# A two-layer transformer forward pass on one core: blocks of the attention's output projection put between the last head's stages, the gating layer's mixing and transposes cut into steps, and its gate vector's products spread over 44 work units instead of 62

## The chip, the core and the metric

The kernel runs on 1 core of one Trainium2 chip. The metric is the device time of one execution in microseconds (us), taken as the median of several runs. The core's engines work at the same time and wait for each other through semaphores: TensorE (PE in the profile, its weight loads PEld) multiplies matrices, VectorE (DVE) and ScalarE (ACT) work element by element, GpSimd (POOL) does a few cross-partition operations, SyncE (SP) issues most DMAs. Matmuls write PSUM; everything else lies in SBUF.

## The reference

256 latent tokens of width 2048 pass two layers. Each layer has a mixer and a feed-forward part; each of the four sub-layers is modulated by six vectors worked out from a condition (`ada_params`) and ends in a gated residual and a layer norm. Layer 0 mixes by neighbourhood attention with 16 heads, layer 1 by the gated MLP below.

```python
def spatial_gating_mlp(a, w_in, ln_g, ln_b, w_s, b_s, w_out):
    u, v = jnp.split(jax.nn.gelu(a @ w_in, approximate=False), 2, axis=-1)
    v = layer_norm(v, ln_g, ln_b).reshape(bsz, n // CHUNK, CHUNK, N_GROUPS, GROUP_DIM)
    v = jnp.einsum("gpq,bkqgc->bkpgc", w_s, v) + jnp.transpose(b_s)[:, :, None]
    return (u * v.reshape(bsz, n, D_MODEL)) @ w_out
...
    sh1, sc1, g1, sh2, sc2, g2 = ada_params(c[:, None, :], ada_w[i], ada_b[i])
    a = modulate(h, sh1, sc1)
...
    h = layer_norm(ALPHA * h + g1 * y, ln_g[i, 0], ln_b[i, 0])
    h = layer_norm(ALPHA * h + g2 * swiglu(modulate(h, sh2, sc2), ffn_w_in[i], ffn_w_out[i]),
                   ln_g[i, 1], ln_b[i, 1])
```

## The kernel before, in words

**Matmuls.** Every large product of 32-bit numbers is made of three matmuls in a rounded 32-bit format (`mm3`, L85 to L88): high part by high part, high by low, low by high. Operands are split into the two parts by an ACT copy (L91) and a DVE subtraction (L92).

**Pieces.** Weights come in pieces of 128x1024 numbers (512 KB). SP issues their DMAs into 4 raw buffers, `prefetch` (L104) splits them (tiles `hw…` and `lw…`) into a ring of 5 buffers from the feed-forward part on, and so the split of a piece stands up to four pieces ahead of its matmuls. One piece feeds 12 matmuls of 128x512. In the gating layer the pieces are named `wg` (two input halves) and `wgo` (output projection), in the feed-forward part `wf` and `wd`, in the attention's output projection `wo`.

**Conditioning tasks.** The vectors from `ada_params` are made in small DVE steps beside the matmuls. A gate vector such as (1, G1), the one that scales the gating layer's output, takes 32 products of 128x1024 on DVE (`gate_task`, L174), each with a 512 KB DMA issued from ACT's queue, and then one `partition_all_reduce` on POOL (`sum_task`, L189) that adds over the 128 partitions. `pace(n)` (L230) spreads the tasks that are queued over n ticks; `block_T` and the output projections call `tick` (L214) once for each piece. A tick with an entry in the list `side` runs that entry and counts 0.3. What is left when the vector is wanted is done at once (`need`, L226).

**Attention (L595 to L604).** After each head's projections its stages (scores, an empty one, transposes, values) wait in the list `pend`; after the last head they are emptied in a row (L603). Then `project_out` (L718) runs the output projection in two halves `nh`; in the first, each piece gives 12 matmuls and a tick.

**Gating layer (L873 to L929).** Four chunks of 8 pieces make v (tiles `gv`), four chunks of 8 pieces make u (tiles `gu`), each chunk through `block_T` (L784) and a Gelu on ACT. Behind chunk nb of u, `spatial` (L896) runs twice for chunk nb-1: four mixing matmuls (L904, tile `sp`), a DVE step on each that adds a bias and multiplies into u (L905), transposes on PE (L909, tile `uvt`) and an ACT copy. The last chunk's two calls are side entries of the output projection `go`. `block_T` takes a list `turn` of extra steps; from its third piece on it runs one behind each piece. The feed-forward part uses that for its own transposes (L819).

A scheduler of the framework reorders independent instructions across and within the engines by its own priorities; the order of the text is where it starts. `keep_in_program_order` fixes the DMAs and the conditioning products.

Of the kernel before, what the change touches and what calls it, by code (L numbers as in the profile page):

```python
# [15 lines left out]
ALU = mybir.AluOpType  # L16
# [3 lines left out]
P = 128  # L20
# [26 lines left out]
W0 = HK0 * P + 512  # L47
EARLY = tuple((3 + 4 * g + h, h, 4 * g) for g in range(3) for h in range(4))
EN = 4
EARLY_END = {HK0 + h: 12 for h in range(4)}  # L50


@with_exitstack
def hybrid_kernel(ctx: ExitStack, tc: tile.TileContext, i, out):
# [175 lines left out]
    def pace(units):  # L230
        state["rate"] = sum(t[1] for t in tasks) / units
# [43 lines left out]
    with tc.tile_pool(name="attnX", bufs=1) as px, ExitStack() as late:  # L275
# [202 lines left out]
        def acc_tile(name):  # L478
            return mp.tile([P, 512], F32, tag="acc", name=name, bufs=4)

        def s_tile(name):
            return mp.tile([P, 512], F32, tag="s", name=name, bufs=2)

        def t_tile(name):
            return mp.tile([P, 512], F32, tag="t", name=name, bufs=2)

        add_tasks(0, SH2, SC2, G1)
        pace(126)
        pend = []
        with tc.tile_pool(name="attnB", bufs=1) as pb:  # L490
            qh, ql = {}, {}

            def advance():
                stage = pend.pop(0)
                if stage:
                    stage()
# [36 lines left out]
            def proj_v(g):  # L533
                ps = [acc_tile(f"vps{g}{b}") for b in range(4)]
                for k2 in range(8):
                    hi, lo = piece()
                    for kk in range(2):
                        kt = k2 * 2 + kk
                        c = slice(kk * 512, (kk + 1) * 512)
                        for b in range(4):  # L540
                            tb = slice(b * P, (b + 1) * P)
                            mm3(ps[b], ah[:, kt, tb], al[:, kt, tb], hi[:, c], lo[:, c], kt == 0, kt == KT - 1)
                    unit(2.0)
                for b in range(4):
                    put_v(g, b, ps[b])
# [49 lines left out]
            for h in range(NH):  # L595
                if h >= HK0:
                    proj_k(h)
                proj_q(h)
                if h in V_AT_Q:
                    while len(pend) > 8:  # L600
                        advance()
                    proj_v(V_AT_Q[h])
            while pend:  # L603
                advance()  # L604

    need((0, SH2), (0, SC2))
    main = ctx.enter_context(tc.tile_pool(name="main", bufs=1))
# [107 lines left out]
    QUIET = 2  # L715
    AHEAD = 400

    def project_out(kts, src, key, name, finish, extra, last=False):  # L718
        st = stats_tile(name)
        hold = LAST if last else HOLD  # L720
        for nh in range(2):
            if nh == 0:
                ps = [[acc_tile(f"po{name}{nh}{n}{b}") for b in range(2)] for n in range(2)]
            else:
                ps = [[s_tile(f"po{name}{nh}0{b}") for b in range(2)]]
                ps.append([acc_tile(f"po{name}{nh}1{b}") for b in range(2)])

            def products(kt, x, w, n, b):
                c, tb = slice(n * 512, (n + 1) * 512), slice(b * P, (b + 1) * P)
                mm3(ps[n][b], x[0][:, tb], x[1][:, tb], w[0][:, c], w[1][:, c], kt == 0, kt == kts - 1)  # L730

            def fetch(kt, n):
                xs = []
                for k in range(n):
                    at = None
                    if k >= START:
                        if k % 2 == 0:
                            e = outer.tile([P, 4, NT], F32R, tag="ada", name=f"e{name}{k}", bufs=ADA)
                        at = e[:, 2 * (k % 2), :], e[:, 2 * (k % 2) + 1, :]
                    xs.append(act_split(src(kt + k), f"{name}{nh}_{kt + k}", at))  # L740
                return xs, take(n)

            k0 = 0
            if nh == 1:
                xs, ws = fetch(0, START)
                for n in range(2):
                    for j in range(START):
                        for b in range(2):
                            products(j, xs[j], ws[j], n, b)
                preload_sqrt(st)  # L750
                k0 = START
            k1 = kts - hold if nh == 1 else kts
            for kt in range(k0, k1):
                if nh == 1 and kt == max(k1 - 9, k0):
                    pos["extra"] = extra()
                w = piece() if nh == 0 or kt < k1 - START else take(1)[0]
                x = act_split(src(kt), f"{name}{nh}_{kt}")
                for n in range(2):
                    for b in range(2):
                        products(kt, x, w, n, b)  # L760
                if nh == 0 or kt < k1 - QUIET:
                    tick()
            if nh == 0:
                need(key)
                g = gate[key]
                for n in range(2):
                    for b in range(2):
                        residual(ps[n][b], b, n, g, st, name)
            else:
                xs, ws = fetch(k1, hold)  # L770
                for b in range(2):
                    for n in range(2):
                        for j in range(hold):
# [34 lines left out]
    def ffn(layer, m, key, name, finish, free, last=False):  # L808
# [45 lines left out]
    project_out(  # L854
        KT, lambda k: oT[:, k, :], (0, G1), "wo", m.first,
        lambda: pw.tile([P, 4, 1024], F32R, tag="w", name="extra_o"),
    )
    affine_tasks(h_t, i["ln_row"][0], "a0")
    add_tasks(0, G2)
# [13 lines left out]
    m = m2[0]  # L873
    affine_tasks(h_t, i["ln_row"][1], "a1")
    add_tasks(1, G1)
    pace(62)
    free = ExitStack()
    pg = free.enter_context(tc.tile_pool(name="gm", bufs=1))
    ws = pg.tile([P, NH, P], F32, tag="ws", name="ws")
# [13 lines left out]
    uT = outer.tile([P, KT, NT], F32, tag="xT", name="uT")  # L893
    us = {}

    def spatial(nb, g2):  # L896
        u = us[nb]
        tp = t_tile(f"uvt{nb}{g2}")
        sp = s_tile(f"sp{nb}{g2}")
        for j in range(2):  # L900
            g = nb * 4 + g2 * 2 + j
            c = slice((g2 * 2 + j) * P, (g2 * 2 + j + 1) * P)
            o = sp[:, j * NT : (j + 1) * NT].rearrange("p (b c) -> p b c", b=2)
            T.matmul(o, ws[:, g, :], vv[:, :, g * P : (g + 1) * P], start=True, stop=True)  # L904
            V.scalar_tensor_tensor(u[:, :, c], o, bs[:, g : g + 1], u[:, :, c], ALU.add, ALU.mult)  # L905
        for j in range(2):
            c = slice((g2 * 2 + j) * P, (g2 * 2 + j + 1) * P)
            for b in range(2):
                T.transpose(tp[:, j * NT + b * P : j * NT + (b + 1) * P], u[:, b, c], ident)  # L909
        S.copy(uT[:, nb * 4 + g2 * 2 : nb * 4 + g2 * 2 + 2, :], tp)  # L910

    for nb in range(NB):
        ps = [acc_tile(f"gu{nb}{b}") for b in range(2)]
        if nb == 0:
            rs = [moments(b, st, "v")[1] for b in range(2)]
            affine_tasks(vv, i["gm_row"], "av", rs)
        block_T(m, ps, False)
        us[nb] = pg.tile([P, 2, 512], F32, tag="u", name=f"u{nb}", bufs=2)
        for b in range(2):
            S.activation(us[nb][:, b, :], ps[b], AF.Gelu)  # L920
        if nb:
            for g2 in range(2):
                spatial(nb - 1, g2)
    side.extend((lambda: spatial(NB - 1, 0), lambda: spatial(NB - 1, 1)))
    m = Modulated(2, 1, SH2, SC2, "f1")
    project_out(
        KT, lambda k: uT[:, k, :], (1, G1), "go", m.first,
# [135 lines left out]
```

## Time and profile before

| | |
|---|---|
| Median of 3 runs | 2418.88 us (2416.48 to 2419.06) |
| The profiled execution's own time | 2419.84 us |
| Its span in the profile | 2418.1 us |
| PE busy | 2381.7 us, 98% |
| DVE busy | 1755.7 us, 73% |
| ACT busy | 1122.7 us, 46% |
| POOL busy | 109.8 us, 5% |

All times are microseconds from the start of the profiled span. In a row of the timeline the first number is the start, the second the duration (for a group the stretch or the sum), then engine, line, operation, output and inputs; behind `x` the number of instructions, and in brackets the idle time of the engine ahead of it and what ended it. Matmuls are pipelined, so the distance between two starts is what one costs. Stages of the gating layer: v from about 1400, its chunks ending at 1411, 1432, 1454 and 1476; u's chunks ending at 1498, 1519, 1548 and 1573; the output projection behind that.

### The profile page before, as it was taken

The numbers are of one execution on the slowest core, as the hardware profiler recorded it, in microseconds if no ns is written. First come the engines' busy times: TensorE is split into PE (matmuls) and PEld (weight loads), VectorE is DVE, ScalarE is ACT, GpSimd is POOL, SyncE is SP. The second block draws the span as 40 slices with busy tenths as digits, with TensorE's granted clock in tenths as the row PEclk, the third lists the DMA queues.
The fourth block names the chain that finished last, engine by engine and source line by source line (L and its number), as shares of the span: only waits on it lengthen the run. The fifth ranks groups of instructions, "written<-read, shape, count | busy, mean of one in ns | idle before, by whom it ended". The sixth has DMA issues, their size and how long they took to land. (4 is left out here: it accounts for less than half of the span.)

```text
span 2418.1 us, 31362 instructions
## 1 busy us (share of the span) xinstructions
PE 2381.7 (98%) x11624; PEld 1977.0 (82%) x11624; DVE 1755.7 (73%) x2155; ACT 1122.7 (46%) x1536; POOL 109.8 (5%) x55
## 2 busy tenths in 40 slices
PE   9999999999999999999999999999999999999998
PEld 6788988888788888888888788777888888888886
DVE  4877867677788877777889788787755555576666
ACT  4344534345644444444445554446544444445553
POOL 0000000020010200000000011020100000020000
PEclk9999999999999999999999999999999999999999
DMA  9977877756679899999989677756766677656563
GB/s 382 346 265 239 272 240 238 244 164 209 197 267 338 302 334 318 320 319 320 329 287 321 202 247 270 271 177 200 235 228 228 226 233 225 207 186 195 176 212 132
DMA packets 167827, 610.64 MB, mean 253 GB/s; under 512 B 19349, under 2 KB 21717, under 8 KB 163317
## 3 DMA queue, kind: packets, MB, share of 16 engines
q1 hardware_dynamic: 121172, 440.74, 54.3%
q10 hardware_dynamic: 46372, 167.86, 20.1%
q8 instruction: 91, 1.49, 0.3%
q14 instruction: 64, 0.52, 0.1%
q0 software_dynamic: 128, 0.03, 0.0%
HBM read 606.46 MB, written 2.10 MB: 252 GB/s over the span
## 5 line engine op out<-in xcount | busy, mean ns | idle before, releaser
L92 DVE TENSOR_TENSOR lwf<-rwf,hwf 128x1024 fp32r<-128x1024 f32 x320 | 407.2, 1275 | 278.9 <-ACT hwf L91 278.6
L91 ACT CAST hwf<-rwf 128x1024 fp32r<-128x1024 f32 x320 | 337.1, 1054 | 490.5 <-PE pu L88 221.6
L86 PE MATMUL pod<-hwd,ghd 128*128 128x512 f32 x684 | 266.4, 390 | 0.0
L87 PE MATMUL pod<-lwd,ghd 128*128 128x512 f32 x684 | 266.2, 389 | 0.0
L88 PE MATMUL pod<-hwd,gld 128*128 128x512 f32 x684 | 265.8, 389 | 0.0
L92 DVE TENSOR_TENSOR lwd<-rwd,hwd 128x1024 fp32r<-128x1024 f32 x172 | 212.2, 1235 | 64.0 <-ACT hwd L91 63.8
L150 DVE SCALAR_TENSOR_TENSOR ad<-ad,c_bc 128x1024 f32<-128x1024 f32 x192 | 232.6, 1219 | 0.6 <-DMA ad<-in_ada_t 0.6
L91 ACT CAST hwd<-rwd 128x1024 fp32r<-128x1024 f32 x172 | 180.6, 1050 | 54.8 <-PE pod L88 28.8
L174 DVE SCALAR_TENSOR_TENSOR gate<-ag,c_col,gate 128x1024 f32<-128x1024 f32 x128 | 163.2, 1282 | 0.0
L88 PEld LDWEIGHTS pod<-hwd,gld 128*128 128x128 f32 x684 | 128.3, 188 | 26.8
L86 PEld LDWEIGHTS pod<-hwd,ghd 128*128 128x128 f32 x684 | 128.4, 188 | 26.7 <-DVE sg L838 0.3
L87 PEld LDWEIGHTS pod<-lwd,ghd 128*128 128x128 f32 x684 | 128.4, 188 | 26.6
L86 PE MATMUL pg<-hwf,f1h 128*128 128x512 f32 x320 | 126.4, 395 | 0.0
L86 PE MATMUL pg<-hwf,f0h 128*128 128x512 f32 x320 | 126.4, 395 | 0.0
L87 PE MATMUL pg<-lwf,f0h 128*128 128x512 f32 x320 | 124.6, 389 | 0.4 <-DVE lwf L92 0.4
L88 PE MATMUL pg<-hwf,f1l 128*128 128x512 f32 x320 | 124.7, 390 | 0.0
L88 PE MATMUL pg<-hwf,f0l 128*128 128x512 f32 x320 | 124.7, 390 | 0.0
L86 PE MATMUL pu<-hwf,f0h 128*128 128x512 f32 x320 | 124.5, 389 | 0.0
L87 PE MATMUL pu<-lwf,f0h 128*128 128x512 f32 x320 | 124.5, 389 | 0.0
L88 PE MATMUL pu<-hwf,f0l 128*128 128x512 f32 x320 | 124.5, 389 | 0.0
L86 PE MATMUL pu<-hwf,f1h 128*128 128x512 f32 x320 | 124.5, 389 | 0.0
L87 PE MATMUL pu<-lwf,f1h 128*128 128x512 f32 x320 | 124.5, 389 | 0.0
(343 smaller groups left out, 5338.5 us busy)
## 6 DMA issues: line engine op xcount, KB each, us to landing
rwf<-in_w_in_t SPq DMA_DIRECT2D x320, 512.0 KB
ad<-in_ada_t ACTq DMA_DIRECT2D x192, 512.0 KB
rwd<-in_w_out SPq DMA_DIRECT2D x176, 512.0 KB
ag<-in_ada_g ACTq DMA_DIRECT2D x128, 512.0 KB
rwg<-in_w_gin SPq DMA_DIRECT2D x64, 512.0 KB
ap<-in_ada_p SPq DMA_DIRECT2D x20, 1024.0 KB
rwq<-in_w_q SPq DMA_DIRECT2D x32, 512.0 KB
rwo<-in_w_o SPq DMA_DIRECT2D x32, 512.0 KB
```

The costliest lines, as they stand in the source:

```text
L86: keep(T.matmul(ps, sh, mh, start=first, stop=False))
L87: keep(T.matmul(ps, sh, ml, start=False, stop=False))
L88: keep(T.matmul(ps, sl, mh, start=False, stop=last))
L91: S.copy(hi, src)
L92: V.tensor_tensor(lo, src, hi.bitcast(F32), ALU.subtract)
L150: pin(V.scalar_tensor_tensor(r, r, 1.0, c_bc[:, half * 1024 : (half + 1) * 1024], ALU.mult, ALU.mult, accum_out=o[:, nt : nt + 1],))
L174: pin(V.scalar_tensor_tensor(g, loaded.pop(key), c_col[:, kt, 0:1], g, ALU.mult, ALU.add))
```

## The change

Three edits. First, the first half of an output projection becomes a pair made by `out_begin` (accumulators, and a step that does one piece), which `project_out` uses for all its callers. For the attention it is made ahead of the place where the last head's stages are emptied: two blocks run when three stages are left and one when one is left (`WHILE`). Second, `spatial` returns four steps, two that mix and two that transpose; they are handed to the `block_T` of the next chunk, so that mixing of chunk nb-1 runs behind pieces 2 and 3 (counted from 0) of chunk nb and the transposes behind pieces 4 and 5, where before both ran behind piece 7. The last chunk's four steps are side entries. Third, the 32 products of gate (1, G1) are paced over 44 units, not 62.

```diff
+WHILE = {3: 2, 1: 1}
...
+        def out_begin(kts, src, name):
+            ps = [[acc_tile(f"po{name}0{n}{b}") for b in range(2)] for n in range(2)]
+
+            def step(kt):
+                w = piece()
+                x = act_split(src(kt), f"{name}0_{kt}")
+                for n in range(2):
+                    c = slice(n * 512, (n + 1) * 512)
+                    for b in range(2):
+                        tb = slice(b * P, (b + 1) * P)
+                        mm3(ps[n][b], x[0][:, tb], x[1][:, tb], w[0][:, c], w[1][:, c], kt == 0, kt == kts - 1)
+                tick()
+
+            return ps, step
...
+            wo_ps, wo_step = out_begin(KT, lambda k: oT[:, k, :], "wo")
+            wo_k = 0
             while pend:
                 advance()
+                for _ in range(WHILE.get(len(pend), 0)):
+                    wo_step(wo_k)
+                    wo_k += 1
...
-                ps = [[acc_tile(f"po{name}{nh}{n}{b}") for b in range(2)] for n in range(2)]
+                ps, step, k0 = begun or (*out_begin(kts, src, name), 0)
+                for kt in range(k0, kts):
+                    step(kt)
...
-    pace(62)
+    pace(44)
...
-    def spatial(nb, g2):
+    def spatial(nb):
         u = us[nb]
...
+        def mix(g2):
+            sp = s_tile(f"sp{nb}{g2}")
...
+                T.matmul(o, ws[:, g, :], vv[:, :, g * P : (g + 1) * P], start=True, stop=True)
+                V.scalar_tensor_tensor(u[:, :, c], o, bs[:, g : g + 1], u[:, :, c], ALU.add, ALU.mult)
+
+        def turn(g2):
+            tp = t_tile(f"uvt{nb}{g2}")
...
+        return [partial(f, g2) for f in (mix, turn) for g2 in range(2)]
...
-        block_T(m, ps, False)
+        block_T(m, ps, False, spatial(nb - 1) if nb else ())
...
-        if nb:
-            for g2 in range(2):
-                spatial(nb - 1, g2)
-    side.extend((lambda: spatial(NB - 1, 0), lambda: spatial(NB - 1, 1)))
+    side.extend(spatial(NB - 1))
```

**First place: DVE in the last chunk of u, with the last products of the gate.** `gate<-ag` is one of the 32 products, `lwg` and `lwgo` are the low parts of pieces, `u<-sp` is the bias and product on a mixed block. Before, DVE's rows from the last piece of that chunk on:

```order
L92 TENSOR_TENSOR lwg_1024_13494<-rwg_1024_13491,hwg_1024_13493 128x1024
L92 TENSOR_TENSOR lwgo_0_0_13512<-rwgo_0_0_13509,hwgo_0_0_13511 128x1024
L174 SCALAR_TENSOR_TENSOR gate_12253<-ag_13306,c_col,gate_12253 128x1024
L92 TENSOR_TENSOR lwgo_0_1024_13533<-rwgo_0_1024_13530,hwgo_0_1024_13532 128x1024
L92 TENSOR_TENSOR lwgo_1_0_13551<-rwgo_1_0_13548,hwgo_1_0_13550 128x1024
L174 SCALAR_TENSOR_TENSOR gate_12253<-ag_13345,c_col,gate_12253 128x1024
L174 SCALAR_TENSOR_TENSOR gate_12253<-ag_13450,c_col,gate_12253 128x1024
L92 TENSOR_TENSOR lwgo_1_1024_13572<-rwgo_1_1024_13569,hwgo_1_1024_13571 128x1024
L905 SCALAR_TENSOR_TENSOR u_13404<-sp_13591,bs,u_13404 128x2x128
L905 SCALAR_TENSOR_TENSOR u_13404<-sp_13602,bs,u_13404 128x2x128
```

Now, the rows from piece 5 of the same chunk on; the gate row among them is the last of the 32:

```order
L93 TENSOR_TENSOR lwg_1024_13474<-rwg_1024_13471,hwg_1024_13473 128x1024
L175 SCALAR_TENSOR_TENSOR gate_12253<-ag_13353,c_col,gate_12253 128x1024
L93 TENSOR_TENSOR lwg_0_13493<-rwg_0_13490,hwg_0_13492 128x1024
L929 SCALAR_TENSOR_TENSOR u_13447<-sp_13508,bs,u_13447 128x2x128
L93 TENSOR_TENSOR lwg_1024_13516<-rwg_1024_13513,hwg_1024_13515 128x1024
L929 SCALAR_TENSOR_TENSOR u_13447<-sp_13508,bs,u_13447 128x2x128
L929 SCALAR_TENSOR_TENSOR u_13447<-sp_13532,bs,u_13447 128x2x128
L93 TENSOR_TENSOR lwgo_0_0_13540<-rwgo_0_0_13537,hwgo_0_0_13539 128x1024
L929 SCALAR_TENSOR_TENSOR u_13447<-sp_13532,bs,u_13447 128x2x128
```

The products of the gate end inside chunk 3 of u now, where before eight more followed in the output projection behind the rows shown; POOL's reduction becomes free to start behind the last one, one low part ahead of the first mixed block's step.

**Second place: PE in the same chunk.** `gu` are the chunk's accumulators, `sp` the mixing matmuls. Now, from the end of piece 2 on:

```order
L89 MATMUL gu_13451<-hwg_0_13412,m1l 128x512
L928 MATMUL sp_13508<-vv,ws 128x256
L87 MATMUL gu_13450<-hwg_1024_13430,m1h 128x512
L88 MATMUL gu_13450<-lwg_1024_13431,m1h 128x512
L89 MATMUL gu_13450<-hwg_1024_13430,m1l 128x512
L928 MATMUL sp_13508<-vv,ws 128x256
L87 MATMUL gu_13450<-hwg_1024_13430,m1h 128x512
```

Before, the mixing of the same chunk stood behind piece 7, at the start of the output projection `pogo`:

```order
L88 MATMUL gu_13430<-hwg_1024_13493,m1l 128x512
L904 MATMUL sp_13591<-vv,ws 128x256
L904 MATMUL sp_13602<-vv,ws 128x256
L86 MATMUL pogo_13618<-hwgo_0_0_13511,ghgo_0_13628 128x512
L904 MATMUL sp_13591<-vv,ws 128x256
L909 MATMUL uvt_13590<-ident,u_13404 128x128 x2
L904 MATMUL sp_13602<-vv,ws 128x256
L909 MATMUL uvt_13601<-ident,u_13404 128x128 x2
```

The second matmul on a tile `sp` writes a tile from which DVE's step on the first has still to read; three long matmuls stand between the two now.

**Third place: PE in the attention's tail.** `pt` are the last head's transposes of its probabilities, `powo` the accumulators of the output projection. Before, in the third block of the projection (the L87 row is of `hwo_1_0`'s block):

```order
L88 MATMUL powo_5242<-hwo_0_1024_5108,glwo_1_5284 128x512
L86 MATMUL powo_5239<-hwo_1_0_5245,ghwo_2_5306 128x512
L575 MATMUL pt_5184<-ident,p_5168 128x128
L575 MATMUL pt_5193<-ident,p_5168 128x128
L87 MATMUL powo_5239<-lwo_1_0_5246,ghwo_2_5306 128x512
L575 MATMUL pt_5184<-ident,p_5180 128x128
```

Now, at the same place:

```order
L89 MATMUL powo_5161<-hwo_0_1024_5108,glwo_1_5217 128x512
L591 MATMUL pt_5233<-ident,p_5172 128x128
L591 MATMUL pt_5233<-ident,p_5184 128x128
L591 MATMUL pt_5233<-ident,p_5172 128x128
L591 MATMUL pt_5233<-ident,p_5184 128x128
L591 MATMUL pt_5242<-ident,p_5172 128x128
L591 MATMUL pt_5242<-ident,p_5184 128x128
L591 MATMUL pt_5242<-ident,p_5172 128x128
L591 MATMUL pt_5242<-ident,p_5184 128x128
L87 MATMUL powo_5158<-hwo_1_0_5190,ghwo_2_5257 128x512
```

Three blocks of the projection stand among the last head's stages in both orders; only the eight transposes have moved together, ahead of the third block.

More of the change, by code (lines that the diff above doesn't have):

```diff
@@ L716, in hybrid_kernel, with project_out @@
     AHEAD = 400
-    def project_out(kts, src, key, name, finish, extra, last=False):
+    def project_out(kts, src, key, name, finish, extra, last=False, begun=None):
         st = stats_tile(name)
@@ L741, in fetch @@
                 return xs, take(n)
-            k0 = 0
             if nh == 1:
@@ L751, in project_out @@
                 k0 = START
-            k1 = kts - hold if nh == 1 else kts
-            for kt in range(k0, k1):
-                if nh == 1 and kt == max(k1 - 9, k0):
+            k1 = kts - hold
+            for kt in range(k0, k1) if nh == 1 else ():
+                if kt == max(k1 - 9, k0):
                     pos["extra"] = extra()
-                w = piece() if nh == 0 or kt < k1 - START else take(1)[0]
+                w = piece() if kt < k1 - START else take(1)[0]
                 x = act_split(src(kt), f"{name}{nh}_{kt}")
@@ L760, in project_out @@
                         products(kt, x, w, n, b)
-                if nh == 0 or kt < k1 - QUIET:
+                if kt < k1 - QUIET:
                     tick()
@@ L856, in hybrid_kernel @@
         lambda: pw.tile([P, 4, 1024], F32R, tag="w", name="extra_o"),
+        begun=(wo_ps, wo_step, wo_k),
     )
@@ L894, in hybrid_kernel @@
     us = {}
-    def spatial(nb, g2):
+    def spatial(nb):
         u = us[nb]
[L898 to L910, printed above, removed]
+        def mix(g2):
+            sp = s_tile(f"sp{nb}{g2}")
+            for j in range(2):
+                g = nb * 4 + g2 * 2 + j
+                c = slice((g2 * 2 + j) * P, (g2 * 2 + j + 1) * P)
+                o = sp[:, j * NT : (j + 1) * NT].rearrange("p (b c) -> p b c", b=2)
+                T.matmul(o, ws[:, g, :], vv[:, :, g * P : (g + 1) * P], start=True, stop=True)
+                V.scalar_tensor_tensor(u[:, :, c], o, bs[:, g : g + 1], u[:, :, c], ALU.add, ALU.mult)
+        def turn(g2):
+            tp = t_tile(f"uvt{nb}{g2}")
+            for j in range(2):
+                c = slice((g2 * 2 + j) * P, (g2 * 2 + j + 1) * P)
+                for b in range(2):
+                    T.transpose(tp[:, j * NT + b * P : j * NT + (b + 1) * P], u[:, b, c], ident)
+            S.copy(uT[:, nb * 4 + g2 * 2 : nb * 4 + g2 * 2 + 2, :], tp)
+        return [partial(f, g2) for f in (mix, turn) for g2 in range(2)]
     for nb in range(NB):
```

## Prediction

> **What bounds the kernel now.** I read the page first, then what PE waits for, then POOL and DVE in order of time.
>
> ```profile
> span 2418.1 us, 31362 instructions
> PE 2381.7 (98%) x11624; PEld 1977.0 (82%) x11624; DVE 1755.7 (73%) x2155; ACT 1122.7 (46%) x1536; POOL 109.8 (5%) x55
> ```
>
> PE works 98% of the span: some 36 us are idle in all. An edit can only win by removing PE waits, or lose by making some. PE's waits, grouped by what is waited for (total, times, longest):
>
> ```profile
> PE pt L575 <- ACT p L565: 3.7, 2, 3.4
> PE pogo L88 <- DVE glgo L92: 2.3, 2, 1.3
> PE sp L904 <- DVE u L905: 2.1, 1, 2.1
> ```
>
> These three are the waits near the edits: 3.7 in the attention's tail, 2.3 in the gating output projection, 2.1 at a mixing matmul. A look at POOL's reductions, each put between the DVE rows that begin about it, shows what is behind two of them:
>
> ```profile
> 528.88 12.24 POOL L189 PARTITION_ALL_REDUCE gate<-gate  x1 [381.68 <-DVE gate L174]
> 530.25 0.43 DVE L558 TENSOR_TENSOR s<-s,bias 128x256 f32<-128x256 f32 x1 [0.88 <-PE s L88]
> 530.59 8.84 DVE L92 TENSOR_TENSOR lwq<-rwq,hwq 128x1024 fp32r<-128x1024 f32 x1
> ...
> 1604.84 1.22 DVE L92 TENSOR_TENSOR lwgo<-rwgo,hwgo 128x1024 fp32r<-128x1024 f32 x1
> 1605.01 12.78 POOL L189 PARTITION_ALL_REDUCE gate<-gate  x1 [101.88 <-DVE gate L174]
> 1606.02 9.30 DVE L92 TENSOR_TENSOR glgo<-uT,ghgo 128x256 fp32r<-128x256 f32 x1
> ...
> 2135.58 1.28 DVE L174 SCALAR_TENSOR_TENSOR gate<-ag,c_col,gate 128x1024 f32<-128x1024 f32 x1
> 2136.95 11.88 POOL L189 PARTITION_ALL_REDUCE gate<-gate  x1 [413.50 <-DVE gate L174]
> 2137.62 9.54 DVE L92 TENSOR_TENSOR lwf<-rwf,hwf 128x1024 fp32r<-128x1024 f32 x1 [0.76 <-ACT hwf L91]
> ```
>
> POOL begins 0.09 behind the end of the last gate product (2135.58 + 1.28 to 2136.95). A DVE subtraction that begins after POOL does not end until 10.2 to 10.6 behind POOL's start (2137.62 + 9.54 − 2136.95 = 10.21; 530.59 + 8.84 − 528.88 = 10.55), where 1.22 is its own time. One that begins 0.17 ahead of POOL (1604.84) takes 1.22, and then the next is held. The bias addition at 530.25, with scores from PSUM and one SBUF tensor, ran in 0.43 while POOL worked. The Trainium skill's page "SBUF — State Buffer", section "Who interferes with whom", states that a DVE instruction with two SBUF inputs and a GpSimd instruction that reads SBUF exclude each other, the first to issue holding the pair for its whole instruction, while a DVE instruction with one SBUF input does not contend. The rows agree, 9.54 held against 0.43 not held.
>
> Such a hold need not reach PE:
>
> ```profile
> 800.00:830.00 30.00, 30.00 (x134) 24.85 (x133) 25.15 (x18) 12.36 (x13) 12.78 (x1) 1.00 0.75 246
> 2130.00:2160.00 30.00, 30.00 (x138) 24.92 (x137) 22.12 (x12) 13.64 (x15) 11.88 (x1) 1.00 0.54 172
> ```
>
> In these two stretches (length, then busy time of PE, PEld, DVE, ACT, POOL), both in a feed-forward part with 12 us of POOL each, PE is busy 30.00 of 30.00: pieces stand up to four ahead, and four are 10.9 of PE (12 matmuls x 0.227 = 2.72 a piece). A hold costs PE only where PE wants something of DVE that isn't prepared so far ahead. That is the question for the change.
>
> **The change part by part.**
>
> *Attention.* The order shows three projection blocks among the last head's stages already; only the eight transposes have moved.
>
> ```profile
> 538.93 0.28 PE L88 MATMUL qps<-ah,lwq 128*128 128x256 f32 x1
> 542.58 0.33 PE L575 MATMUL pt<-ident,p 128*128 128x128 f32 x1 [3.37 <-ACT p L565]
> ...
> 546.03 0.41 PE L86 MATMUL qps<-ah,hwq 128*128 128x256 f32 x1
> 546.24 0.41 PE L87 MATMUL qps<-al,hwq 128*128 128x256 f32 x1
> ...
> 546.64 0.27 PE L86 MATMUL qps<-ah,hwq 128*128 128x256 f32 x1
> 546.76 0.28 PE L87 MATMUL qps<-al,hwq 128*128 128x256 f32 x1
> ```
>
> The 3.37 wait stands ahead of the last head's query matmuls (`qps`, 546), so it belongs to the head before; it follows from the hold at 530.59, and the edit does not reach it. Where the transposes stood among the blocks there was no wait:
>
> ```profile
> 558.10 0.87 PE L575 MATMUL pt<-ident,p 128*128 128x128 f32 x6
> 558.73 0.47 PE L88 MATMUL powo<-hwo,glwo 128*128 128x512 f32 x1
> ```
>
> Six transposes took 558.73 − 558.10 = 0.63 and nothing idles around them. I take 0; at most the 0.3 that remains of the 3.7 goes, or as much comes.
>
> One more thing is in the six rows above: behind the hole, 256-column matmuls start 0.21 apart up to 546.24 and 0.12 apart from 546.64 on. So a hole of 3.4 is followed by about 546.64 − 542.58 = 4.06 of reduced pace, worth 4.06 x (1 − 0.12/0.21) = 1.7 more.
>
> *The reduction in u's chunk 3 (pace 44).* The last gate product now stands there, between the low parts of pieces 5 and 6, and behind piece 6's comes the first mixed block's step `u`, for which PE's second mixing matmul waits. Before, the same chunk with its gate products ran like this:
>
> ```profile
> 1557.30 1.23 DVE L92 TENSOR_TENSOR lwg<-rwg,hwg 128x1024 fp32r<-128x1024 f32 x1 [1.50 <-ACT hwg L91]
> 1558.44 1.28 DVE L174 SCALAR_TENSOR_TENSOR gate<-ag,c_col,gate 128x1024 f32<-128x1024 f32 x1
> 1558.69 0.39 PE L86 MATMUL gu<-hwg,m1h 128*128 128x512 f32 x1
> 1560.02 1.23 DVE L92 TENSOR_TENSOR lwg<-rwg,hwg 128x1024 fp32r<-128x1024 f32 x1 [0.30 <-ACT hwg L91]
> ```
>
> Let L be the start of piece 5's low part. The gate product begins at L+1.14 and ends at L+2.42; POOL starts 0.09 later, P = L+2.51. Piece 6's low part begins when its copy is there, L+2.72 = P+0.21: after POOL, so it is held until P+10.21 (by the row of 2137.62, the nearest: the same operation, 0.67 after POOL). Then `u`, 0.43:
>
> ```profile
> 1519.29 1.03 PE L904 MATMUL sp<-vv,ws 128*128 128x256 f32 x4
> 1519.97 0.58 PE L86 MATMUL gu<-hwg,m1h 128*128 128x512 f32 x1
> 1522.33 0.87 DVE L905 SCALAR_TENSOR_TENSOR u<-sp,bs,u 128x256 f32<-128x256 f32 x2
> 1522.86 1.22 PE L904 MATMUL sp<-vv,ws 128*128 128x256 f32 x2 [2.08 <-DVE u L905]
> 1525.87 0.64 PE L88 MATMUL gu<-hwg,m1l 128*128 128x512 f32 x1
> 1526.34 0.40 PE L86 MATMUL gu<-hwg,m1h 128*128 128x512 f32 x1
> 1526.58 0.39 PE L87 MATMUL gu<-lwg,m1h 128*128 128x512 f32 x1
> ```
>
> `u` is there at P+10.64. When does PE want it? Piece 6's copy follows the start of piece 2 on PE (1558.69 to 1560.02: 1.33 ahead of its low part), so piece 3 starts at P+0.21−1.33+2.72 = P+1.60. One mixing matmul is 0.34 ((1519.97 − 1519.29)/2), three long ones are 0.68, and the second is due at P+2.62. PE waits 10.64 − 2.62 = 8.0, and with 1.7 of reduced pace behind it loses 9.7. By the Trainium skill's rule ("SBUF — State Buffer", "Who interferes with whom") the first to issue keeps the pair for its whole instruction, which would be up to 12.78 by POOL's rows, a wait of 12.78 + 0.43 − 2.62 = 10.6 and a sum of +11.3, an estimate; the held rows end at 10.21 to 10.55, and the sum goes by them.
>
> What hid the hold in the feed-forward part doesn't hide this: there PE wanted pieces, four ahead; here it wants `u` within 2.6. The low end: if DVE runs late, piece 6's low part begins ahead of POOL and isn't held, `u` runs as the bias addition did, and piece 7's low part is the held one. Then the second pair waits. Its `u` is due 9 long matmuls, a mixing one, three more long ones and one 0.34 later (2.04 + 0.34 + 0.68 + 0.34 = 3.4): 8.0 − 3.4 = 4.6, with the reduced pace 6.3. The lowest is 0, if nothing waits.
>
> *The first mixing (chunk 1).* It stood behind piece 7 and cost PE the 2.08 and, by the starts from 1522.86 to 1526.58, half pace up to 1526.34, about half of 3.5, together 3.8. Now it is behind pieces 2 and 3, close to the affine steps on v:
>
> ```profile
> 1507.00 0.68 DVE L661 TENSOR_TENSOR vv<-vv,lrav 128x512 f32<-128x512 f32 x1
> 1507.60 1.22 DVE L92 TENSOR_TENSOR lwg<-rwg,hwg 128x1024 fp32r<-128x1024 f32 x1
> 1508.73 1.28 DVE L174 SCALAR_TENSOR_TENSOR gate<-ag,c_col,gate 128x1024 f32<-128x1024 f32 x1
> 1509.93 1.22 DVE L92 TENSOR_TENSOR lwg<-rwg,hwg 128x1024 fp32r<-128x1024 f32 x1
> ```
>
> By these starts a low part takes 1.13 and a gate product 1.20 of DVE. In the order of the change three low parts (pieces 4 to 6) and two gate products stand between the last `vv` and the first `u`; before, piece 4's stood ahead of the last `vv`, which so ends 1.13 earlier, at 1506.5, if nothing else delays it. `u` is done at 1506.5 + 3 x 1.13 + 2 x 1.20 + 0.43 = 1512.7. PE reached piece 3 at 1519.29 − 5 x 2.72 = 1505.69; between it and the second matmul on the first `sp` tile the order has a mixing matmul, piece 3, a mixing matmul and one long one, so that is due 0.34 + 2.72 + 0.34 + 0.23 later, at 1509.3. It waits 3.4, and with 1.7 of pace loses 5.1, against 3.8 before: +1.3. One more gate product in front of `vv` makes that +2.5. At best the wait vanishes, −3.8, if `vv` ends 3.4 earlier still.
>
> *The output projection.* DVE's backlog at 1605 to 1615 goes away with the eight gate products and the reduction; so do the 2.3 of waits: −2.3. The cover is that nothing else of DVE's piles up there.
>
> *Gate products earlier.* From v's chunks on, 32/44 of a product a tick instead of 32/62.
>
> ```profile
> 1410.00:1435.00 25.00, 25.00 (x112) 20.68 (x111) 24.30 (x27) 12.96 (x14) 8.33 (x7) 1.00 0.67 214
> ```
>
> In v's chunk 1 DVE is busy 24.30 of 25.00 and PE 25.00. One or two more products (1.2 each) fall here and would be covered by the pieces ahead; 0, at worst 1.5.
>
> Sum: +9.7 + 1.3 − 2.3 = +8.7. The profiled execution took 2419.84 (span 2418.1), 0.96 over the median, 2418.88; on the median that is 2427.6.
>
> **The rivals.** *The later step is held* (`u` ahead, piece 7 held): 6.3 + 1.3 − 2.3 = +5.3, 2424.2. It decides if piece 6's low part begins over 0.21 earlier than reckoned; the 0.30 of idle time ahead of it at 1560.02 speaks against. *The reduction is hidden* as in the feed-forward part: if the gate's last product ends so late or early that no `u` stands behind the held step within 10, the first term is gone: +1.3 − 2.3 = −1.0, 2417.9, not slower. For it: two reductions of four cost PE nothing. Against: the order has `u` directly behind. *Hidden, and the first mixing freed* too: DVE has caught up with vv by 1509: −3.8 − 2.3 = −6.1, 2412.8, faster. *Only the first mixing is freed*: 9.7 − 3.8 − 2.3 = +3.6, 2422.5. *DVE too late in v* as well: +1.5 and one more hole of the 3.8 at 1522, 2427.6 + 1.5 + 3.8 = 2432.9. That the attention edit would do what its name says and remove a wait is answered by the order: what it asks for stood there.
>
> **How the numbers follow.** A measurement of this kernel can tell some 0.2%, 4.84, from no change: the bounds are 2414.0 and 2423.7. Chances: forecast 0.49 and later step held 0.19, both slower; DVE too late 0.03, slower; hidden 0.13 and only the first freed 0.07, both the same; hidden and first freed 0.09, faster. Slower 0.71, same 0.20, faster 0.09. The range leaves out the faster case and 2432.9 (0.12 together), and takes in the hidden case, 2417.9, with the best of the attention and an untouched pace behind it (1.4 less: 2416.5), and the forecast with one more gate product ahead of `vv` (+1.2), v's 1.5, the 0.3 of the attention and a hold of 10.55 instead of 10.21: 2431.0. So 2416.5 to 2431. The forecast's own range, with the pace behind the wait left out at its low end, is 2425.9 to 2431.
>
> **What would show it right or wrong.** Right: POOL's third reduction near 1557 (not 1605), a low part `lwg` of 8 to 10 behind it, and a wait of PE at `sp` on `u` of 5 to 8; no wait at `pogo` on `glgo`; the 3.4 at `pt` still there; the first `sp` wait of 2 to 5 near 1510. Wrong: PE busy all through the reduction; `u` itself ahead of POOL; or a loss in v's chunks or at the transposes of the last head.

## The result, and the profile after

The change is slower: 2430.83 us in the median of 4 runs (2429.01 to 2433.29), before 2417.78; the ratio is 1.0051, 95% interval 1.0036 to 1.0067. The forecast was 2427.6 with a range of 2416.5 to 2431. Of all executions told below one, the profiled one of the kernel with a pause of gate products, ran at a granted clock of 0.85 and took 2644 us; it is left out, and that kernel has no rows to compare.

The page's span and busy line, and those of PE's waits that changed or that the forecast named (total, times, longest):

```profile
span 2431.5 us, 31378 instructions
PE 2381.1 (98%) x11624; PEld 1975.6 (81%) x11624; DVE 1756.7 (72%) x2155; ACT 1121.0 (46%) x1536; POOL 108.0 (4%) x55
...
PE sp L928 <- DVE u L929: 14.4, 2, 7.8
PE pt L591 <- ACT p L581: 3.4, 1, 3.4
PE gv L88 <- DVE lwg L93: 1.6, 1, 1.6
PE gu L88 <- DVE lwg L93: 1.6, 2, 0.9
```

PE does the same work, 2381 us, and the span is 13.4 longer. The wait on `u` was 2.1 and is 14.4, in two holes; `pogo` on `glgo` (2.3 before) is gone from the list; `pt` has kept its 3.4; the waits on low parts `lwg`, one in v and two in u, are new.

The larger hole, in u's chunk 3. Rows of POOL, DVE and PE in order of time (`...` stands for rows left out), where the tile `gate` is the gate vector and `u` the mixed block's step:

```profile
1562.84 1.28 DVE L175 SCALAR_TENSOR_TENSOR gate<-ag,c_col,gate 128x1024 f32<-128x1024 f32 x1
1564.22 11.88 POOL L190 PARTITION_ALL_REDUCE gate<-gate  x1 [54.14 <-DVE gate L175]
1564.33 10.09 DVE L93 TENSOR_TENSOR lwg<-rwg,hwg 128x1024 fp32r<-128x1024 f32 x1 [0.21 <-ACT hwg L92]
...
1574.34 0.47 DVE L929 SCALAR_TENSOR_TENSOR u<-sp,bs,u 128x256 f32<-128x256 f32 x1
1574.87 1.22 PE L928 MATMUL sp<-vv,ws 128*128 128x256 f32 x2 [7.80 <-DVE u L929]
...
1576.32 0.63 PE L88 MATMUL gu<-lwg,m1h 128*128 128x512 f32 x1
1576.74 0.63 PE L89 MATMUL gu<-hwg,m1l 128*128 128x512 f32 x1
```

POOL starts 0.10 behind the last product, the low part of piece 6 starts 0.11 behind POOL and ends 10.20 behind POOL's start (1564.33 + 10.09 − 1564.22); `u` follows, and PE has waited 7.80. Then matmuls start 0.42 apart instead of 0.227. The clock in this stretch and in the one behind the other hole (length; busy PE, PEld, DVE, ACT, POOL; granted clock, DMA share, GB/s) is half:

```profile
1574.80:1579.70 4.90, 4.83 (x11) 3.85 (x12) 1.63 (x3) 0.00 (x0) 1.29 (x1) 0.50 0.66 215
1518.50:1521.90 3.40, 3.36 (x8) 2.70 (x9) 3.21 (x5) 0.38 (x1) 0.00 (x0) 0.50 0.94 274
```

The other hole, at the first mixing in u's chunk 1, with the last steps on v (`vv`) ahead of it:

```profile
1506.86 0.60 PE L928 MATMUL sp<-vv,ws 128*128 128x256 f32 x2
...
1511.01 1.28 DVE L682 TENSOR_TENSOR vv<-vv,lrav 128x512 f32<-128x512 f32 x2
1512.21 1.21 DVE L93 TENSOR_TENSOR lwg<-rwg,hwg 128x1024 fp32r<-128x1024 f32 x1
1513.35 1.27 DVE L175 SCALAR_TENSOR_TENSOR gate<-ag,c_col,gate 128x1024 f32<-128x1024 f32 x1
1514.55 1.21 DVE L93 TENSOR_TENSOR lwg<-rwg,hwg 128x1024 fp32r<-128x1024 f32 x1
1515.68 1.27 DVE L175 SCALAR_TENSOR_TENSOR gate<-ag,c_col,gate 128x1024 f32<-128x1024 f32 x1
1516.88 1.21 DVE L93 TENSOR_TENSOR lwg<-rwg,hwg 128x1024 fp32r<-128x1024 f32 x1
1518.01 0.47 DVE L929 SCALAR_TENSOR_TENSOR u<-sp,bs,u 128x256 f32<-128x256 f32 x1
...
1518.54 1.22 PE L928 MATMUL sp<-vv,ws 128*128 128x256 f32 x2 [6.55 <-DVE u L929]
```

From the last `vv` (free at 1512.21) to the end of `u` at 1518.48 DVE works without a gap, 6.3. PE wanted `u` some 6.5 earlier.

To compare whole stretches I add up how far the starts of PE's matmuls lie apart beyond 0.227 for 512 columns, 0.215 for a mixing matmul's record and 0.113 for a transpose. This counts holes and reduced pace together. The columns are stretches of 20 us or multiples, in microseconds of each profiled span; the kernels of the lower rows are told below.

| Loss of PE, us | 1420–1440 | 1480–1500 | 1500–1540 | 1560–1600 | 1600–1660 | 1660–1700 |
|---|---|---|---|---|---|---|
| before | 0.0 | 0.0 | 4.0 | 0.8 | 2.8 | 6.3 |
| after | 1.9 | 1.0 | 9.7 | 10.9 | 0.4 | 5.1 |
| steps and blocks, pace 62 | 0.2 | 0.0 | 5.0 | 0.8 | 6.4 | 5.1 |
| pace 44 alone | 0.7 | 0.0 | 7.0 | 3.6 | 0.0 | 5.1 |
| last product later | 0.8 | 0.0 | 8.7 | 2.3 | 0.4 | 6.4 |
| no reduction | 2.4 | 0.3 | 10.9 | 0.6 | 0.0 | 9.2 |

### The profile page after: what moved, and what is told of

Same layout as the page of the kernel before. It is cut to its first block, busy times and chain, and to the rows that moved or that the text cites. A ratio compares the mean times of both kernels' runs of the same rounds, so it can differ in the third digit from the quotient of the medians.

```text
span 2431.5 us, 31378 instructions
## 1 busy us (share of the span) xinstructions
PE 2381.1 (98%) x11624; PEld 1975.6 (81%) x11624; DVE 1756.7 (72%) x2155; ACT 1121.0 (46%) x1536; POOL 108.0 (4%) x55
## 5 line engine op out<-in xcount | busy, mean ns | idle before, releaser
L87 PE MATMUL pod<-hwd,ghd 128*128 128x512 f32 x684 | 266.4, 390 | 0.0
L87 PEld LDWEIGHTS pod<-hwd,ghd 128*128 128x128 f32 x684 | 128.4, 188 | 26.8 <-DVE sg L860 0.3
L87 PE MATMUL pg<-hwf,f0h 128*128 128x512 f32 x320 | 126.4, 395 | 0.0
L87 PE MATMUL pg<-hwf,f1h 128*128 128x512 f32 x320 | 126.4, 395 | 0.0
L87 PE MATMUL pu<-hwf,f0h 128*128 128x512 f32 x320 | 124.5, 389 | 0.0
L87 PE MATMUL pu<-hwf,f1h 128*128 128x512 f32 x320 | 124.5, 389 | 0.0
```

The costliest lines, as they stand in the source:

```text
L87: keep(T.matmul(ps, sh, mh, start=first, stop=False))
```

## The experiments

The theory: POOL's reduction, which now starts ahead of the third mixing's `u`, holds the low part in front of it, and earlier gate products put DVE behind ahead of the first mixing. The rival: the steps stand too early, whatever the gate does. Times are medians, ratios are to the kernel before on the same chip.

**Steps and blocks, but pace 62.**

```diff
-    pace(44)
+    pace(62)
```

> The changed kernel with the gate paced over 62 units again; blocks and steps stay. Theory (the earlier gate products both delay the affine steps on v ahead of the first mixing and put POOL's reduction ahead of the third mixing's u): the reduction is back in the output projection and costs about 2.6 there, the 7.8 wait of PE at the third mixing and its reduced pace (together 10.7) are gone, the 1.9 in v's chunk 2 and the 0.9 at 1489 too, and the first mixing loses about 5 instead of 10: 2430.8 - 10.7 - 1.9 - 0.9 - 5 + 2.6, about 2415. Rival (the first mixing's hole comes from the place of the steps alone, not from the gate products): the hole of 10 at the first mixing stays, 2420 to 2423.

2419.17 us, ratio 1.0012 (1.0002 to 1.0021); the changed kernel had 1.0051. Its waits:

```profile
PE pogo L89 <- DVE glgo L93: 4.3, 2, 3.3
...
PE sp L928 <- DVE u L929: 2.8, 1, 2.8
```

The 7.8 is gone and the first mixing waits 2.8, not 6.6, at the same place: the rival falls. The time is 4 above the expectation; the stretch of the reduction (1611.72) in the output projection lost 6.4 and not 2.6, with two waits of which the longer is 3.3.

**The kernel before with pace 44 alone.** The edit is the same line the other way.

> The kernel before with the gate paced over 44 units, nothing else. Theory: the last gate product is in u's chunk 3 with only low parts of pieces behind it, so the reduction is hidden by the pieces ahead and PE loses nothing there; the 2.6 in the output projection go, v's chunk 2 loses about 1.9, and the first mixing, behind piece 7 of chunk 1, waits longer than the 2.1 of before since the affine steps on v end later: by 2 to 5. Together 2417.8 - 2.6 + 1.9 + (2 to 5), 2419 to 2422. Rival (a reduction in u's chunk 3 costs PE its 8 wherever the mixing stands): 2427 to 2430. Rival (the first mixing's hole is due to the steps' place alone): 2417.

2421.36 us, 1.0014 (1.0005 to 1.0024). The reduction fell into u's chunk 3 here too, with low parts alone behind it:

```profile
1559.28 11.14 DVE L92 TENSOR_TENSOR lwg<-rwg,hwg 128x1024 fp32r<-128x1024 f32 x2 [0.30 <-ACT hwg L91]
1570.34 2.35 DVE L92 TENSOR_TENSOR lwgo<-rwgo,hwgo 128x1024 fp32r<-128x1024 f32 x2
```

Two low parts took 11.14, so one of them was held for about 10, as in the changed kernel, and PE lost 3.6 in the stretch, not 10.9. The hold is the same, with no `u` directly behind it. Of the 3.6, 2.1 is again a wait on a `u`, that of the third mixing behind piece 7 (1578.05), but there DVE had stood idle 1.29 and 1.17 ahead of low parts since the hold; how much of the 3.6 is the hold's isn't shown. The first mixing waited 2.03, no longer than before and not the 2 to 5 more that were expected; the 3 more between 1500 and 1540 are waits on low parts (`gu` on `lwg`: 2.3 in two) and the reduced pace behind them.

So on the same base (2417): pace alone +4.0 (by the interval of its ratio 1.2 to 5.8), steps and blocks alone +1.8 (0.5 to 5.1), both +13.1 (8.7 to 16.2).

**Without the blocks between the last head's stages.**

```diff
-WHILE = {3: 2, 1: 1}
+WHILE = {}
...
-        begun=(wo_ps, wo_step, wo_k),
```

> The changed kernel without blocks of the output projection written between the last head's stages; steps and pace as changed. Theory (three blocks stood there before too, put there by the scheduler): within 1 of the changed kernel, 2430 to 2432, with the 3.4 wait at pt in the head before. Rival (writing the blocks there removes or makes a wait in the tail): 2 or more away from it, with the difference between 526 and 562 in the trace.

2431.19 us, 1.0061 (1.0046 to 1.0076), 0.4 from the changed kernel, and the wait at `pt` is there in both. That edit is worth nothing that can be measured, as the order had it.

**The last gate product three ticks later**, the other 31 and all steps as changed (a product's cost in units is 0.5; the pace keeps their rate):

```diff
-        return [(layer, t), 0.5, run, fetch]
+        last = (layer, t, kt, half) == (1, G1, KT - 1, 1)
+        return [(layer, t), LATE if last else 0.5, run, fetch]
...
+LATE = 1.625
...
-    pace(44)
+    pace(47)
```

> The changed kernel with the last of the 32 gate products three ticks later, the other 31 where they were: it now stands behind the third mixing's four u. Theory (the hole at the third mixing is the low part held by POOL's reduction ahead of u): the 7.8 wait and its pace (10.7) are gone, and the reduction, which then holds a low part of the output projection's pieces, is hidden by the pieces ahead or costs at most 2: 2420 to 2422, with the hole at the first mixing unchanged (6.6 wait). Rival (u waits for DVE's queue of low parts at that place, reduction or not): the wait at the third mixing stays, 2429 to 2431.

2423.96 us, 1.0028 (1.0018 to 1.0039). DVE at the third mixing and behind it:

```profile
1558.31 1.22 DVE L94 TENSOR_TENSOR lwg<-rwg,hwg 128x1024 fp32r<-128x1024 f32 x1 [1.40 <-ACT hwg L93]
1560.39 0.48 DVE L931 SCALAR_TENSOR_TENSOR u<-sp,bs,u 128x256 f32<-128x256 f32 x1 [0.85 <-PE sp L930]
...
1566.36 1.28 DVE L176 SCALAR_TENSOR_TENSOR gate<-ag,c_col,gate 128x1024 f32<-128x1024 f32 x1
1568.61 11.60 DVE L94 TENSOR_TENSOR lwgo<-rwgo,hwgo 128x1024 fp32r<-128x1024 f32 x3 [0.97 <-ACT hwgo L93]
```

The low part ahead of `u` takes 1.22, DVE waits for PE there and not PE for DVE. The held group of three took 11.60 and PE lost 2.3 in that stretch, 1.4 of it in a wait on the `u` of the next mixing, which DVE reached late behind that group. The time is 2 above the expectation. One product moved by three pieces is worth between 6 and 7 of the 13.

**Without the reduction of gate (1, G1).** It leaves out that vector's sum over the partitions, and nothing else.

```diff
-            nc.gpsimd.partition_all_reduce(g, g, P, ReduceOp.add)
+            if (layer, t) != (1, G1):
+                nc.gpsimd.partition_all_reduce(g, g, P, ReduceOp.add)
```

> The changed kernel without POOL's reduction of gate (1, G1): the sum over partitions is left out. Theory (the low part ahead of the third mixing's u is held by that reduction, and by nothing else): that low part takes 1.2 instead of 10.1, PE doesn't wait at the third mixing, the first mixing keeps its wait of 6.6: 2430.8 - 10.7, about 2420. Rival (the hold is of the DMAs or the raw buffers behind the low part): the wait stays.

2423.81 us, 1.0024 (1.0012 to 1.0036), 7.0 below the changed kernel and 4 above the expectation. The same two rows as in the changed kernel, with the same idle time ahead of the second:

```profile
1562.36 1.28 DVE L175 SCALAR_TENSOR_TENSOR gate<-ag,c_col,gate 128x1024 f32<-128x1024 f32 x1
1563.85 1.23 DVE L93 TENSOR_TENSOR lwg<-rwg,hwg 128x1024 fp32r<-128x1024 f32 x1 [0.21 <-ACT hwg L92]
```

10.09 became 1.23: the hold is POOL's reduction. The table shows the 10.3 gained at 1560 to 1600, and 4.1 given back at 1660 to 1700, where the feed-forward part begins; the other wait there, `pg` on the low part of its own input, 1.8, is new. Why that stretch differs between two kernels that are equal up to there but for the reduction stays open.

**The first mixing: place, normalisation, rows.** Five kernels tried what makes DVE late there. All but one start from the kernel with the last product later. The first puts chunk 1's steps behind pieces 5 to 7:

```diff
-            if turn and k2 >= 2:
+            if turn and k2 >= at:
                 turn.pop(0)()
+        while turn:
+            turn.pop(0)()
...
-        block_T(m, ps, False, spatial(nb - 1) if nb else ())
+        block_T(m, ps, False, spatial(nb - 1) if nb else (), 5 if nb == 1 else 2)
```

> The run with the last gate product later, and besides the first mixing's steps (chunk 1 only) behind pieces 5 to 7 instead of 2 to 5. Theory (DVE is behind, and stays so while a low part and nearly one gate product come with each piece: 2.33 of 2.72): three more low parts and three more gate products now stand ahead of the first u, 7.0, and PE wants it about 7.2 later, so most of the wait of 6.4 at the first mixing stays, 5 to 6.4, and the time is within 2 of that run, 2422 to 2425. Rival (it is only the place, too close behind the affine steps): with 7 more of time the wait falls below 1 and the time to 2414 to 2417.

2421.25 us, 1.0018 (1.0009 to 1.0027), and these waits:

```profile
PE sp L933 <- DVE u L934: 4.2, 2, 2.7
PE gu L90 <- DVE lwg L95: 3.6, 3, 1.9
```

At the mixing 2.7 is left of 6.4, less than the theory had, but PE now waits for low parts instead, and by the measure of the table the stretch 1500 to 1540 lost 8.7 as with the last product later alone: DVE is behind by then (busy 10.00 of 10.00 from 1496 to 1506 and from 1506 to 1516), and its lateness shows wherever PE next wants something. The second moves v's normalisation, eight steps, from DVE to ACT:

```diff
-                    normalise(t3, b, nb, rs[b])
+                    S.activation(t3[:, b, sl], t3[:, b, sl], AF.Identity, bias=rs[b][:, 1:2], scale=rs[b][:, 0:1])
```

> The run with the last gate product later, and besides the normalisation of v (8 steps, 0.46 each from start to start on DVE) on ACT. Theory (DVE's backlog ahead of the first mixing is what PE waits for): 3.7 fewer on DVE, so the wait of 6.4 there falls to about 2.7 and the time by 4 to 5, to 2419 to 2420. Rival (the affine steps are late because of POOL's broadcasts and their DMAs, not of DVE's work): the wait stays above 5.

2421.61 us, 1.0018 (1.0008 to 1.0027), and the wait stays 6.6: its rival holds. DVE has gaps, and a row vector from POOL ends some of them:

```profile
1506.30 1.63 DVE L683 TENSOR_TENSOR vv<-vv,lrav 128x512 f32<-128x512 f32 x2 [0.70 <-POOL lrav L82]
```

Three rows of SP's queue from this kernel, where a pair of rows (`lrav`) is fetched:

```profile
1487.99 1.99 SPq L81 DMA_DIRECT2D lrav<-in_gm_row  x2
1494.40 1.46 SPq L81 DMA_DIRECT2D lrav<-in_gm_row  x2
1500.99 1.46 SPq L81 DMA_DIRECT2D lrav<-in_gm_row  x2
```

They lie 6.4 and 6.6 apart with the normalisation away. There are two buffers for rows, so a row can be fetched only once an earlier one is used, and a late start is passed on to the last pair. In the changed kernel, gate products ran right ahead of v's statistics, and the second pair was fetched at 1491.23:

```profile
1479.78 1.28 DVE L175 SCALAR_TENSOR_TENSOR gate<-ag,c_col,gate 128x1024 f32<-128x1024 f32 x1
1480.97 1.22 DVE L93 TENSOR_TENSOR lwg<-rwg,hwg 128x1024 fp32r<-128x1024 f32 x1
1482.11 0.69 DVE L915 BATCH_NORM_STATS2 stv<-vv 128x6 f32<-128x512 f32 x1
...
1491.23 1.99 SPq L80 DMA_DIRECT2D lrav<-in_gm_row  x2
```

In the kernel before it was fetched at 1485.47:

```profile
1485.47 1.98 SPq L79 DMA_DIRECT2D lrav<-in_gm_row  x2
```

That is 5.8 later, where PE's piece 3 of chunk 1 was 1.2 later (1506.86 for 1505.69): 4.6 of lateness that stand already at the second pair, as much as `vv` is in the end later than I worked out (5.4 behind the mixing's first matmul, for 0.8). Whether all of it comes from the gate products was tried only through the pace.

The third adds a pause of gate products during these steps to the second (a tick with a side entry gives no units in u's chunk 0; the last product costs 1.0, the pace is 45.33).

> As the run with v's normalisation on ACT, and besides no gate products during the eight affine steps on v, with the last product again behind the third mixing's u. Theory: at least two products (2.4) fewer ahead of the first mixing, so the wait there is 0 to 0.5; no wait at the third mixing; the reduction mostly hidden: about 2.5 below the run with v's normalisation on ACT, 2414 to 2417, below the kernel before. Rival (the products only move and DVE is short further on): a wait of 2 or more at the second or third mixing, and no gain.

2426.93 us in the median of five, 1.0039 (1.0025 to 1.0053), a miss by 10 whose cause stays open. The fourth and fifth give the rows four buffers (`bufs=4` for the tag `zt`) with the normalisation on ACT, once with the last product later, once at pace 62:

> The run with v's normalisation on ACT and the last gate product later, and besides four buffers for the row vectors that the affine steps multiply and add, instead of two. Theory (two limits share the affine steps on v: DVE's backlog, and a ring of two row buffers in which a pair of rows is fetched, spread over the partitions by POOL and used before the next can start, 6.4 to 6.8 from issue to issue at 1491.23, 1498.03, 1504.55; taking away one leaves the other): with both away v's last step ends at least 4 earlier, PE's wait of 6.6 at the first mixing falls below 2.5, and the time by 4 to 8, to 2414 to 2418. Rival (gate products and low parts alone fill DVE, rows have no part): the wait stays above 5 and the time within 2.

> The run with the gate paced over 62 units again (blocks and steps of the change), with the four row buffers and v's normalisation on ACT. Theory: the wait of 2.8 at its first mixing is gone (it loses 4.7 to 5 there), the 4.3 at pogo on glgo behind the reduction stay: 2414 to 2416, below the kernel before. Rival (DVE's order ahead of the first u decides, not v): the wait stays at 2 to 3 and the time at 2418 to 2420.

2427.22 us, 1.0046 (1.0032 to 1.006), and 2432.12 us, 1.0065 (1.0052 to 1.0077). At the mixing the waits fell: the longest is 3.7 for 6.6 (below 2.5 was expected), and 0.8 for 2.8. Both times are misses, by 9 and by 16. The tag serves the affine steps on h and the modulated blocks too, in three other stages, and there PE has new waits. The second of the two kernels:

```profile
PE pu L88 <- DVE lwt L93: 3.5, 2, 2.6
...
PE sp L928 <- DVE u L929: 0.8, 1, 0.8
```

The first wait is new, as is one of 1.4 on `lwg` in v. Rows of DVE and PE at the longest of them, where `lra` are the rows for h:

```profile
672.76 2.10 DVE L682 TENSOR_TENSOR h_t<-h_t,lra 128x512 f32<-128x512 f32 x2 [1.33 <-POOL lra L81]
...
675.84 3.95 DVE L93 TENSOR_TENSOR lwt<-rwt,hwt 128x1024 fp32r<-128x1024 f32 x3
677.11 0.79 PE L88 MATMUL pu<-lwt,f0h 128*128 128x512 f32 x1 [2.56 <-DVE lwt L93]
```

DVE isn't short of time here: it stands idle for a row from POOL, and the low parts, of which ACT's copies were there from 667.33 on, are queued behind the step that wants the row. In this profile the three stages (600 to 700, 1400 to 1420, 1700 to 1730) lost some 7 more than at pace 62 alone, and the first mixing 3.3 less; that leaves most of the 13 between the medians unexplained. Buffers for the gating rows alone weren't tried.

**Two mixtures**, both with chunk 1's steps behind pieces 5 to 7 and the normalisation on ACT: one with the last product later, one at pace 56.

> The run with the last gate product later and the first mixing's steps behind pieces 5 to 7, and besides v's normalisation on ACT (row buffers two as before). Theory (DVE's backlog at 1504 to 1510 made PE wait for low parts of pieces there, 3.6 in all, and 2.7 for u): 3.7 less of DVE work ahead of it takes away most of both: 2415 to 2418. Rival (the ring of two row buffers holds the affine steps back by as much): the waits stay and the time at 2420 to 2422.

> Steps and blocks of the change with the gate paced over 56 units, the first mixing's steps behind pieces 5 to 7, v's normalisation on ACT. Theory: with some 3 gate products fewer ahead of the first mixing than at 44 and 3.7 of DVE work less, no wait at any mixing; the reduction falls into the output projection, where the low parts of its left operand are made one or two pieces ahead, and costs 2 to 4 there: 2412 to 2415, below the kernel before. Rival (one of the moved steps still finds DVE behind): a wait of 2 or more at sp, 2417 or above.

2420.99 us, 1.0017 (1.0008 to 1.0026), and 2416.95 us, 0.9999 (0.999 to 1.0008). The first still waits 4.7 at a mixing, the second 3.7, with 1.0 at `pogo`: the rival of each holds. The second equals the kernel before; none of the runs is faster than it.

## Why the prediction was right, and where its sizes were off

*The reduction in chunk 3*, +9.7 by the sum: measured 10.1 more in the stretch 1560 to 1600 (10.9 less 0.8). Every step of it shows in the rows: POOL 0.10 behind the last product (0.09), the low part held until 10.20 behind POOL's start (10.21), the wait 7.80 (8.0). The reduced pace behind it was longer than I took: half clock for 4.9, some 2.4 lost for 1.7. Both the run without the reduction and the one with the last product later remove the hold, so this cause is shown. By the Trainium skill, page "SBUF — State Buffer", section "Who interferes with whom", whoever issues first gets the shared port pair for the whole instruction (the page says this of DVE's modes with two ports). Here the held low part was done at 10.20, ahead of the end of POOL's row at 11.88, so the sum with the measured 10.21 was the nearer.

*The first mixing*, +1.3: measured 5.7 more (9.7 less 4.0), above my worst of +2.5. The step that failed is "which so ends 1.13 earlier, at 1506.5, if nothing else delays it". The last `vv` ended at 1512.2, 5.4 behind the mixing's first matmul, where I had it 0.8 behind. I counted the gate products behind `vv` and put those ahead of it in the bound as one more; in the trace others stand right ahead of v's statistics and the ring of row buffers passed the lateness on to the last pair; that these products are the whole cause isn't shown. The step count behind `vv`, three low parts and two products, was right: 6.3 to the end of `u`, worked out 6.2.

*The output projection*, −2.3: measured −2.4. *Gate products in v*, 0 with 1.5 at worst: 1.9, and 1.0 more at 1480 to 1500; the pieces ahead did not cover them, and this term should not have been 0. Its size isn't steady: the eight comparable profiles with pace 44 or 47 and the old row buffers lost 0.3 to 2.8 at 1420 to 1440. *The attention*, 0: 0.4, by the run without the blocks, within the noise.

The terms as measured, 10.1 + 5.7 − 2.4 + 2.9, make 16.3, and the span grew by 13.4. The profiled execution after was early by 2.8 from its start on (the first reduction at 526.11 for 528.88; 526.48 with pace 44 alone, where the attention is untouched), so that is not the change's doing. It was also the slowest of the four, 2.5 above their median. The forecast of +8.7, for +13.1 of the medians, was low by the first mixing and v's stage. With a first mixing outside its own bound, that the time came out 0.2 inside the range is partly luck. Of the rivals, the reduction hidden as in the feed-forward part came nearest to being true in the kernel with pace 44 alone, where no `u` stands directly behind the held step: that stretch lost 3.6 and not 10.9.

## What to carry to other kernels

A hold costs what is queued behind it on the engine, so a POOL reduction is placed by what DVE owes next: with low parts of pieces directly behind it, its stretch of the gating layer lost 2 to 4 here, in part by a later `u`, and 10.9 with a `u` directly behind that PE wanted within 3. In front of the left operand `glgo` of the output projection it was 2.8 and 6.4. Two edits that are each near neutral (+4.0 and +1.8) can meet in one queue and cost 13; compare the order of both together before they are made together. Where DVE is more than nine tenths busy, as around the first mixing (38.50 of 40.00 from 1476 to 1516), moving a late step further back moved the wait to the next thing that PE wanted (8.7 lost with and without); fewer products ahead helped more (5.0 at pace 62).

## What the runs showed of the hardware beyond what I expected

The hold goes with POOL's row. In all profiles a held low part of 128x1024 ended 1.7 ahead of the end of that row: 10.2 behind POOL's start where the row lasts 11.88 (here, and at 2136.95 before), 10.55 where it lasts 12.24 (528.88 before), 11.1 where it lasts 12.78 (811.99 before). Whether DVE is let go before POOL is done, or the row is longer than the work, the rows don't tell. The longer rows are those of reductions that started 0.18 behind the start of a DVE subtraction, which ended 0.50 and 1.04 behind POOL's start; so there POOL seems to be the one that waited first.

The granted clock falls and rises on a grid. In every trace the stretches of half clock inside the kernel last 3.41, 6.83 or 10.24 and start whole multiples of 3.41 apart. In the changed kernel they run from 1515.12 to 1521.95 and from 1569.74 to 1579.98, so they begin inside the holes, where they cost nothing, and 3.4 and 5.1 are left behind them. The same hole of 6.5 at the first mixing was followed by 3.2 of half clock without the blocks, 3.4 in the changed kernel and 6.1 without the reduction: where a hole falls on the grid counts, and not its length alone. From 10 us on, every step of the grid with 1.9 or more of idle PE was followed by one of half clock, and none that had full clock and up to 1.5; so the hole of 2.08 at 1522.86 before was enough.

Two kernels with four row buffers for two came out slower: steps that wait for a row from POOL then stood ahead of low parts in DVE's order. In the one profile read for it that is some 7 of loss; the rest stays open.
